# A decoder trunk on one core: the substitution of the delta rule's block inverses on the vector engine, and X without its mask

## The chip, the cores and the metric

The kernel runs on one core of one Trainium2 chip. The metric is the device time of one execution in microseconds; the runs of the kernel before are given by their median. The engines have short names throughout: PE is TensorE (PEld its weight loads), DVE is VectorE, ACT is ScalarE, POOL is GpSimd, SP is SyncE, whose queue issues the DMAs here.

## The reference

Two layers over 1024 tokens of 1024 features, all in float32. Layer 0 mixes tokens by a Conformer convolution (pointwise products with a gate, a causal depthwise convolution of width 31, a layer norm, a pointwise product), layer 1 by a gated DeltaNet with 8 heads of 128. After each mixer comes a squared-relu MLP with 4096 hidden features. Each part is preceded by an RMS norm, and one norm ends the whole. The change touches the delta rule of layer 1, which in the reference goes by chunks of 64 tokens:

```python
decay = jnp.exp(jnp.where(causal, g[..., :, None] - g[..., None, :], -jnp.inf))
k_beta = k * beta[..., None]
kk = jnp.einsum('bhnid,bhnjd->bhnij', k_beta, k) * decay
m = jnp.where(strict, kk, 0.0) + jnp.eye(CHUNK, dtype=jnp.float32)
rhs = jnp.concatenate([v * beta[..., None], k_beta * jnp.exp(g)[..., None]], axis=-1)
sol = lax.linalg.triangular_solve(m, rhs, left_side=True, lower=True, unit_diagonal=True)
```

`m` is 1 plus a strictly lower triangular matrix; the kernel forms its inverse instead of solving.

## The kernel before

The tokens go in two halves of 512. Activations lie with features on the partitions, 8 tiles of 128 x 512 to a half. A dense product (`product`, L164) takes 24 matmuls of 128 x 512: weights and activations are each the sum of two float32r parts, high and low, and three of the four combinations are added up (L178 to L180). Weights come from DRAM by SP (L130), ACT rounds the high part (L138, `wh`), and DVE subtracts to get the low one (L139, `wl`). This is done for every one of the 376 or so products, two ahead of their use.

The delta rule is work beside the products. It is written as generators that are advanced one step at every `tick()` inside and between the products: `gdn` runs `delta(hf, h0, yo)` for a pair of heads at a time, two streams of pairs, the second 40 steps behind the first, four pairs to a half. In the first half it goes beside the head projections (`gdn_in`) and the MLP of layer 0's second half, in the second half beside the projections and the MLP of layer 1's first half. The chunk here is 128 tokens, so a pair has 8 chunks (`NU`), each with a 128 x 128 matrix X.

What a pair does, in the names that the text uses:

- k and q are loaded (`ld`, DRAM tiles `sc` written by `gin`); sums of squares go to columns of `cl`.
- `e` is exp(-|difference of decay sums|) (L699 to L703, from `gr`, a load of the decay sums). POOL multiplies `e` by a strictly triangular mask into `el` (L706, `tril`) and by the other triangle in place (L708, `triu`).
- `X` is k times k, from PSUM, scaled and multiplied by `el` on DVE (L717). Its 32 x 32 diagonal blocks go to DRAM (`xd`, L722). `AT` (L731) is the same for q times k with `e`; POOL multiplies q by exp of the decays (L729, `qe`).
- The substitution: the 32 diagonal blocks of a pair are loaded with a block to a partition (`fx`, L742; `ft` begins as the identity, L743 and L744), and 31 steps on POOL turn `ft` into their inverses:

```python
for j in range(31):
    sh = [NU * 4, 31 - j, j + 1]
    nc.gpsimd.tensor_tensor(out=fm, in0=fx[:, j + 1:, j:j + 1].to_broadcast(sh),
                            in1=ft[:, j:j + 1, 0:j + 1].to_broadcast(sh), op=ALU.mult)
    nc.gpsimd.tensor_tensor(out=ft[:, j + 1:, 0:j + 1], in0=ft[:, j + 1:, 0:j + 1],
                            in1=fm, op=ALU.subtract)
```

- One pair is inverted at a time (the list `inverting`). `ft` goes to DRAM (`td`, L760) and comes back as `T` with rows on the partitions (L763). DVE transposes T's blocks (`ub`, L773) and copies them into `U` (L782, cleared before by POOL in L779). Matmuls y (L789, L798, L818, L825) make the rest of the 128 x 128 inverse from X, U and T, with copies of T by POOL (`t6s`, L811 to L813).
- The scan over the chunks (L832 on: `pk`, `R`, `py`, `ys`, `po`, `pS`, `st`) and the gated norm of the output, to DRAM (`yo`).

Every engine has one queue, and SP's queue issues all DMAs in order. The order in each queue isn't that of the source: a planner simulates a timeline of all engines from a cost for each instruction, with priorities by the order of the source (weights go 300 places earlier, `PRIO`), and writes the order down. On the chip each queue then keeps it, whatever the true durations are. Tiles come from pools with a fixed number of buffers; `g_tile` has 27.

Of the kernel before, what the change touches and what calls it, by code (L numbers as in the profile page):

```python
# [17 lines left out]
KC = D // P            # feature chunks  # L18
HT = S // 2            # tokens of a half
NCH = HT // P          # chunks of the delta rule in a half  # L20
H = 8                  # heads
NQ = 4                 # parts of the hidden layer
# [3 lines left out]
HG = 2                 # heads that go through the delta rule together  # L26
# how each tile of the depthwise convolution is done, by half (v: the vector engine, a: ScalarE
# and Pool, p: Pool, s: the vector engine but for the last SHARED taps), and how many taps go
# between two steps
# [3 lines left out]
INV = 5                # steps from the inverses to what uses them  # L33
IJ = 3                 # steps of the substitution traced at a time
LANE = 40              # steps by which the second stream of heads is behind
AHEAD = 2              # products whose weights are under way
PRIO = 300             # by how much weights go before what was traced earlier
HB = 10                # tiles in the pools
AB = 17
GB = 27  # L40
NB = 6                 # conv tiles of the second half before the first half's layer norm
# norms whose sum of squares goes to TensorE as two float32r parts
# [9 lines left out]
def _body(ctx, tc, a, out):  # L52
# [12 lines left out]
    def const(shape, name, val=None, dt=F32):  # L65
        t = cp.tile(shape, dt, tag=name, name=name)
        if val is not None:
# [10 lines left out]
    # [t, j] = 1 where t <= j, and its strict transpose  # L78
# [3 lines left out]
    tril = const([P, P], "tril")  # L82
    nc.gpsimd.affine_select(out=tril, in_=ones, pattern=[[-1, P]], compare_op=ALU.is_ge,
                            fill=0.0, base=-1, channel_multiplier=1)
# [13 lines left out]
    def split(dst, src):  # L98
        """src as the sum of two float32r parts"""
        nc.scalar.activation(out=dst[:, 0, :], in_=src, func=AF.Copy)  # L100
        nc.vector.tensor_tensor(out=dst[:, 1, :], in0=src, in1=dst[:, 0, :].bitcast(F32),  # L101
                                op=ALU.subtract)
# [7 lines left out]
    # weights that stay for a second pass over them  # L110
    keep = [f"m2_11_{NQ - 1}{o}" for o in range(KC)]

    def weights(src, name, n=KC * P):
        """weights as the sum of two float32r parts"""
        if n < KC * P:
            # few columns: both parts side by side
            raw = wp.tile([P, KC * P], F32, tag="raw", name=f"raw_{name}")
            nc.sync.dma_start(raw[:, :n], src)
            r3 = raw[:, :n].rearrange("p (k m) -> p k m", k=KC)
            both = wp.tile([P, KC * P], F32R, tag="wh", name=f"wh_{name}")  # L120
            b4 = both.rearrange("p (k i m) -> p k i m", k=KC, i=2)
            nc.scalar.activation(out=b4[:, :, 0], in_=r3, func=AF.Copy)
            nc.vector.tensor_tensor(out=b4[:, :, 1], in0=r3, in1=b4[:, :, 0].bitcast(F32),
                                    op=ALU.subtract)
            return both, None
        raw = wp.tile([P, KC * P], F32, tag="raw", name=f"raw_{name}")
        # the first ones in parts, so that the products start early
        n = KC * P // (2 if name in ("pa0_0", "pb0_0") else 1)
        for c in range(0, KC * P, n):
            nc.sync.dma_start(raw[:, c:c + n], src[:, c:c + n])  # L130
        kept = name in keep
        wh = wp.tile([P, KC * P], F32R, tag="kh" if kept else "wh", name=f"wh_{name}",
                     bufs=KC if kept else 2)
        wl = wp.tile([P, KC * P], F32R, tag="kl" if kept else "wl", name=f"wl_{name}",
                     bufs=KC if kept else 2)
        for c in range(0, KC * P, n):
            s = slice(c, c + n)
            nc.scalar.activation(out=wh[:, s], in_=raw[:, s], func=AF.Copy)  # L138
            nc.vector.tensor_tensor(out=wl[:, s], in0=raw[:, s], in1=wh[:, s].bitcast(F32),  # L139
                                    op=ALU.subtract)  # L140
        return wh, wl

    # work that goes on beside the products: it is traced in steps between them
# [41 lines left out]
    # the products in their order; weights are fetched and split one product ahead  # L185
# [38 lines left out]
    def add_stats(ps, x, first=True, last=True):  # L224
        """means over the features, with the tokens on the partitions, a chunk to a column"""
# [4 lines left out]
    def rstd_of_tokens(ps, name):  # L230
        """1 / sqrt(mean + eps) from such means, for all partitions with the tokens along them"""
# [26 lines left out]
    def norm(get, g, name, act, eng=nc.vector):  # L258
        """rms_norm of the half, split for the products, into act"""
# [13 lines left out]
    def norm_later(get, g, name, act):  # L273
        """rms_norm of the half but for 1 / rms, split into act; that factor is made meanwhile"""
# [88 lines left out]
    def own_taps(hf, ct):  # L363
        """how many taps of the tile are the vector engine's"""
        return {"v": CW, "s": CW - SHARED}.get(CONV[hf][ct][0], 0)
# [17 lines left out]
    def conv_pool(hf):  # L383
        """the taps that Pool adds up, by itself or from ScalarE's products"""
# [25 lines left out]
    def conv_vec(hf):  # L410
        """the vector engine's taps; the sum so far is in PSUM"""
# [27 lines left out]
    def layer_norm(hf, act):  # L439
# [8 lines left out]
        for k in range(KC):  # L448
            nc.vector.tensor_tensor(out=c[k], in0=c[k], in1=mu, op=ALU.subtract)
            sq = squares(c[k], f"ln{hf}{k}")  # L450
            # sums of two, or of all in the second half where TensorE has other work
# [57 lines left out]
    def mlp_out_last(l, hf, hid, q):  # L509
        """the end of the work: by quarters of the tokens, so that little is left after the last"""  # L510
# [38 lines left out]
    def ab(hf, act):  # L549
        """decays and betas of the half, tokens on partitions"""  # L550
        ps = dense(act, f"ab{hf}", 64)
        # rows 64.. have the share of the weights' low parts
# [15 lines left out]
        # what 1 + e rounded away  # L568
# [26 lines left out]
        # the sums of the decays with tokens along the row, for each head, in DRAM  # L595
# [8 lines left out]
    def gin(hf, act, h):  # L604
        """projections of a head, the short convolution, silu; to DRAM"""
# [38 lines left out]
    def delta(hf, h0, yo):  # L644
        """the delta rule for heads h0.. of the half; gated and normalised output into yo"""
# [44 lines left out]
        for i, h in enumerate(hh):  # L690
            # sums of the decays, the same on all partitions
# [12 lines left out]
            el = g_tile(f"el{nm}{h}")[:, :HT]  # L704
            el3 = el.rearrange("p (c d) -> p c d", c=NCH)
            nc.gpsimd.tensor_tensor(out=el3, in0=e3,  # L706
                                    in1=tril.unsqueeze(1).to_broadcast([P, NCH, P]), op=ALU.mult)
            nc.gpsimd.tensor_tensor(out=e3, in0=e3,  # L708
                                    in1=triu.unsqueeze(1).to_broadcast([P, NCH, P]), op=ALU.mult)
# [5 lines left out]
            X[h] = g_tile(f"X{nm}{h}")[:, :HT].rearrange("p (c d) -> p c d", c=NCH)  # L715
            for c in range(NCH):
                nc.vector.scalar_tensor_tensor(out=X[h][:, c, :], in0=g1[:, c, :],  # L717
                                               scalar=sk2[:, i, c:c + 1], in1=el3[:, c, :],
                                               op0=ALU.mult, op1=ALU.mult)
            for b in range(4):  # L720
# [18 lines left out]
        # inverses of the 32 x 32 diagonal blocks of 1 + X, a block to a partition  # L739
# [5 lines left out]
        for j in range(31):  # L745
# [3 lines left out]
            nc.gpsimd.tensor_tensor(out=fm, in0=fx[:, j + 1:, j:j + 1].to_broadcast(sh),  # L749
                                    in1=ft[:, j:j + 1, 0:j + 1].to_broadcast(sh), op=ALU.mult)  # L750
            nc.gpsimd.tensor_tensor(out=ft[:, j + 1:, 0:j + 1], in0=ft[:, j + 1:, 0:j + 1],  # L751
# [23 lines left out]
        # U is the transpose of the whole inverse: block by block  # L775
# [32 lines left out]
        # the inverse of the upper left quarter, not transposed  # L808
# [21 lines left out]
        # the scan  # L830
# [36 lines left out]
        # o is short of the factor rq / sqrt(dk); rec holds its square  # L867
# [42 lines left out]
    def final(hf, cols=slice(0, HT)):  # L910
# [18 lines left out]
        for k in range(KC):  # L929
            y = g_tile(f"fo{nm}{k}")[:, :n]  # L930
            if cols.start and k % 3 == 1:
                # the last ones are shared with Pool
# [21 lines left out]
    def gdn(hf, ready, yo, lane):  # L954
        """every other group of heads, once it has its inputs"""
# [87 lines left out]
def order(a):  # L1043
    """the products' names and weights, in their order"""
# [33 lines left out]
def arrange(i):  # L1078
    import numpy as np

    def cols(x):
        """[n * 128] -> [128, n]"""
        return np.asarray(x).reshape(-1, P).T
# [6 lines left out]
    def tiles(w):  # L1090
        """[K, N] -> [K / 1024 * N / 128, 128, 1024]: weights of 128 columns and 1024 rows"""
# [54 lines left out]
```

## Time and profile before

| | us |
|---|---|
| median of 3 runs | 2451.02 |
| lowest and highest run | 2450.73, 2455.44 |
| profiled execution, first to last instruction | 2454.3 |
| PE busy | 2333.6 |
| DVE busy | 1529.1 |
| ACT busy | 1082.7 |
| POOL busy | 973.5 |

The profile is of one execution, whose span is 3.3 us above the median of the runs. Lines named L are those of the kernel before. A row of a timeline gives the start, the duration, the engine, the line, the operation, what it writes and reads, and in brackets how long the engine was idle before it and what ended that.

### The profile page before, as it was taken

Reading aid. Unit: us, or ns where it says so; the run is one execution under the profiler, and the core shown is the slowest. Engines: PE = TensorE matmul, PEld = TensorE weight load, DVE = VectorE, ACT = ScalarE, POOL = GpSimd, SP = SyncE. Lnnn points to the kernel's source line nnn. Section 1 sums busy time; section 2 is a strip of 40 time slices with the busy share of each in tenths; the row PEclk is TensorE's granted clock in tenths of the full one; section 3 lists DMA queues with packets and bytes.
Section 4 is the critical chain, followed back from the end, with each engine's and each line's share of the span. In section 5 each row is a group of like instructions: output and inputs, shape, how many; then the busy total and the mean of one; then the engine's idle time right before and its main releaser. Section 6 shows DMA issues by size and latency. Waiting matters only on the chain. (4 is left out here: it accounts for less than half of the span.)

```text
span 2454.3 us, 30203 instructions
## 1 busy us (share of the span) xinstructions
PE 2333.6 (95%) x11412; PEld 1922.2 (78%) x11412; DVE 1529.1 (62%) x2166; ACT 1082.7 (44%) x1549; POOL 973.5 (40%) x945
## 2 busy tenths in 40 slices
PE   8798799999999989999999999899999999999998
PEld 6576677888778868888888888678888888788888
DVE  8998989645768765654435588656454346533334
ACT  6764442343536544443424365434334244432432
POOL 6898299999400557264300004571634000000000
PEclk9899899999999989999999999899999999999999
DMA  5222123333434533433325445334333243433332
GB/s 171 82 82 82 52 86 88 101 90 102 124 119 150 172 101 111 141 114 100 95 85 184 128 140 179 97 109 129 109 111 100 85 154 112 126 98 102 95 103 78
DMA packets 112962, 275.38 MB, mean 112 GB/s; under 512 B 28656, under 2 KB 30896, under 8 KB 112816
## 3 DMA queue, kind: packets, MB, share of 16 engines
q1 hardware_dynamic: 112816, 273.46, 36.6%
q8 instruction: 89, 1.46, 0.2%
q14 instruction: 57, 0.47, 0.1%
HBM read 241.92 MB, written 31.49 MB: 111 GB/s over the span
## 5 line engine op out<-in xcount | busy, mean ns | idle before, releaser
L138 ACT ACTIVATE wh_m<-raw_m 128x1024 fp32r<-128x1024 f32 x256 | 271.0, 1060 | 752.5 <-PE ps_m L179 698.0
L139 DVE TENSOR_TENSOR wl_m<-raw_m,wh_m 128x1024 fp32r<-128x1024 f32 x256 | 327.6, 1281 | 246.8 <-ACT wh_m L138 245.8
L180 PE MATMUL ps_m<-hid,wl_m 128*128 128x512 f32 (+1 forms) x1088 | 411.9, 380 | 6.8 <-DVE wl_m L139 6.8
L178 PE MATMUL ps_m<-hid,wh_m 128*128 128x512 f32 (+1 forms) x1088 | 413.5, 381 | 2.5 <-DVE xo L530 1.0
L179 PE MATMUL ps_m<-hid,wh_m 128*128 128x512 f32 (+1 forms) x1088 | 411.3, 379 | 0.0
L402 POOL TENSOR_TENSOR cp<-cp,cv 128x512 f32<-128x512 f32 x202 | 314.9, 1570 | 16.5 <-ACT cv L400 10.4
L180 PEld LDWEIGHTS ps_m<-hid,wl_m 128*128 128x128 f32 x1088 | 205.3, 189 | 47.2 <-DVE wl_m L139 10.5
L178 PEld LDWEIGHTS ps_m<-hid,wh_m 128*128 128x128 f32 x1088 | 205.3, 189 | 40.7 <-ACT wh_m L138 3.2
L179 PEld LDWEIGHTS ps_m<-hid,wh_m 128*128 128x128 f32 x1088 | 205.2, 189 | 37.0 <-issue 0.2
L935 POOL TENSOR_TENSOR fof<-fof,rstd_f 128x256 f32<-128x256 f32 x3 | 2.6, 890 | 567.8 <-DVE rstd_f L928 567.8
L729 POOL TENSOR_TENSOR ld<-qe,ld 128x512 f32<-128x512 f32 x16 | 21.7, 1356 | 482.3 <-ACT qe L696 254.2
L180 PE MATMUL ps_m<-xn_a,wl_m 128*128 128x512 f32 x512 | 202.9, 397 | 8.5 <-DVE wl_m L139 8.5
L180 PE MATMUL ps_m<-xn_b,wl_m 128*128 128x512 f32 x512 | 200.9, 393 | 5.9 <-DVE wl_m L139 5.9
L178 PE MATMUL ps_m<-xn_a,wh_m 128*128 128x512 f32 x512 | 201.9, 394 | 1.2 <-ACT wh_m L138 1.2
L178 PE MATMUL ps_m<-xn_b,wh_m 128*128 128x512 f32 x512 | 201.7, 394 | 1.0 <-ACT wh_m L138 1.0
L179 PE MATMUL ps_m<-xn_a,wh_m 128*128 128x512 f32 x512 | 201.3, 393 | 0.0
L179 PE MATMUL ps_m<-xn_b,wh_m 128*128 128x512 f32 x512 | 200.7, 392 | 0.0
L427 DVE SCALAR_TENSOR_TENSOR ca<-u,vec,ca 128x512 f32<-128x512 f32 x268 | 188.3, 745 | 0.5
L749 POOL TENSOR_TENSOR fm<-fx,ft 32x31 f32<-32x31 f32 (+15 forms) x248 | 163.6, 660 | 59.5 <-DMA fx<-xd 40.7
L751 POOL TENSOR_TENSOR ft<-ft,fm 32x31 f32<-32x31 f32 (+15 forms) x248 | 169.5, 683 | 19.4
L397 POOL TENSOR_SCALAR cv<-u,vec 128x512 f32<-128x512 f32 x90 | 174.2, 1943 | 0.0
L101 DVE TENSOR_TENSOR hid<-mt,hid 128x512 fp32r<-128x512 f32 x128 | 95.7, 748 | 48.4 <-ACT hid L100 48.2
(348 smaller groups left out, 4851.7 us busy)
## 6 DMA issues: line engine op xcount, KB each, us to landing
raw_m<-w SPq DMA_DIRECT2D x256, 512.0 KB, 3.6
raw_in<-w_in SPq DMA_DIRECT2D x64, 512.0 KB, 3.6
sc<-iy SPq DMA_DIRECT2D x64, 256.0 KB, 2.2
ld<-sc SPq DMA_DIRECT2D x64, 256.0 KB, 4.1
raw_p<-w_pw SPq DMA_DIRECT2D x16, 512.0 KB, 3.6
raw_go<-w_out SPq DMA_DIRECT2D x16, 512.0 KB, 3.6
raw_pa<-w_pw SPq DMA_DIRECT2D x15, 512.0 KB, 3.6
raw_pb<-w_pw SPq DMA_DIRECT2D x15, 512.0 KB, 3.6
```

What stands on the lines that cost most here:

```text
L101: nc.vector.tensor_tensor(out=dst[:, 1, :], in0=src, in1=dst[:, 0, :].bitcast(F32), op=ALU.subtract)
L138: nc.scalar.activation(out=wh[:, s], in_=raw[:, s], func=AF.Copy)
L139: nc.vector.tensor_tensor(out=wl[:, s], in0=raw[:, s], in1=wh[:, s].bitcast(F32), op=ALU.subtract)
L178: nc.tensor.matmul(o, wh[:, s], hi, start=(k == 0), stop=False)
L179: nc.tensor.matmul(o, wh[:, s], lo, start=False, stop=False)
L180: nc.tensor.matmul(o, wl[:, s], hi, start=False, stop=last)
L397: nc.gpsimd.tensor_scalar(out=t, in0=u[:, j:j + HT], scalar1=tap(ct, j), scalar2=None, op0=ALU.mult)
L402: nc.gpsimd.tensor_tensor(out=c, in0=c, in1=t, op=ALU.add)
L427: nc.vector.scalar_tensor_tensor(out=c if j == CW - 1 else acc, in0=u[:, j:j + HT], scalar=tap(ct, j), in1=acc, op0=ALU.mult, op1=ALU.add)
L729: nc.gpsimd.tensor_tensor(out=qT[h], in0=qe, in1=qT[h], op=ALU.mult)
L749: nc.gpsimd.tensor_tensor(out=fm, in0=fx[:, j + 1:, j:j + 1].to_broadcast(sh), in1=ft[:, j:j + 1, 0:j + 1].to_broadcast(sh), op=ALU.mult)
L751: nc.gpsimd.tensor_tensor(out=ft[:, j + 1:, 0:j + 1], in0=ft[:, j + 1:, 0:j + 1], in1=fm, op=ALU.subtract)
```

## The change

The two instructions of each substitution step are given to DVE. The mask `tril` and the tile `el` go: X is formed with `e` itself, and the multiplication by `triu`, which is done in place, comes after X in the source. Comments and docstrings go too.

```diff
-    tril = const([P, P], "tril")
-    nc.gpsimd.affine_select(out=tril, in_=ones, pattern=[[-1, P]], compare_op=ALU.is_ge,
-                            fill=0.0, base=-1, channel_multiplier=1)
...
             nc.scalar.activation(out=e, in_=e, func=AF.Exp, scale=-1.0)
-            el = g_tile(f"el{nm}{h}")[:, :HT]
-            el3 = el.rearrange("p (c d) -> p c d", c=NCH)
-            nc.gpsimd.tensor_tensor(out=el3, in0=e3,
-                                    in1=tril.unsqueeze(1).to_broadcast([P, NCH, P]), op=ALU.mult)
-            nc.gpsimd.tensor_tensor(out=e3, in0=e3,
-                                    in1=triu.unsqueeze(1).to_broadcast([P, NCH, P]), op=ALU.mult)
             yield
...
             for c in range(NCH):
                 nc.vector.scalar_tensor_tensor(out=X[h][:, c, :], in0=g1[:, c, :],
-                                               scalar=sk2[:, i, c:c + 1], in1=el3[:, c, :],
+                                               scalar=sk2[:, i, c:c + 1], in1=e3[:, c, :],
                                                op0=ALU.mult, op1=ALU.mult)
+            nc.gpsimd.tensor_tensor(out=e3, in0=e3,
+                                    in1=triu.unsqueeze(1).to_broadcast([P, NCH, P]), op=ALU.mult)
...
-            nc.gpsimd.tensor_tensor(out=fm, in0=fx[:, j + 1:, j:j + 1].to_broadcast(sh),
+            nc.vector.tensor_tensor(out=fm, in0=fx[:, j + 1:, j:j + 1].to_broadcast(sh),
                                     in1=ft[:, j:j + 1, 0:j + 1].to_broadcast(sh), op=ALU.mult)
-            nc.gpsimd.tensor_tensor(out=ft[:, j + 1:, 0:j + 1], in0=ft[:, j + 1:, 0:j + 1],
+            nc.vector.tensor_tensor(out=ft[:, j + 1:, 0:j + 1], in0=ft[:, j + 1:, 0:j + 1],
                                     in1=fm, op=ALU.subtract)
```

## Rows read from the trace of the kernel before

**Rows 1.** The page's first part: busy time, share of the span and number of instructions of each engine.

```profile
PE 2333.6 (95%) x11412; PEld 1922.2 (78%) x11412; DVE 1529.1 (62%) x2166; ACT 1082.7 (44%) x1549; POOL 973.5 (40%) x945
```

**Rows 2.** Waits of PE from 780 to 1250 us, longest first: who waited for whom, us in total, times, longest.

```profile
PE y L789 <- DVE U L782: 11.3, 1, 11.3
PE ps_m L180 <- DVE wl_m L139: 5.9, 3, 2.7
```

**Rows 3.** The same from 1530 to 1970 us.

```profile
PE y L789 <- DVE U L782: 10.6, 1, 10.6
PE ps_m L180 <- DVE wl_m L139: 8.3, 2, 5.7
PE py L849 <- DVE R L844: 2.0, 1, 2.0
```

**Rows 4.** Timeline of POOL from 832 to 890 us: the first substitution's first and last instruction (62 in all) and what follows.

```profile
832.74 0.25 POOL L749 TENSOR_TENSOR fm<-fx,ft 32x31 f32<-32x31 f32 x1 [9.04 <-DMA fx<-xd]
...
883.15 0.24 POOL L751 TENSOR_TENSOR ft<-ft,fm 32x31 f32<-32x31 f32 x1
...
886.38 1.25 POOL L706 TENSOR_TENSOR el<-e,tril 128x512 f32<-128x512 f32 x1
```

**Rows 5.** Timeline of DVE from 872 to 893 us.

```profile
887.67 1.12 DVE L717 SCALAR_TENSOR_TENSOR X<-g,cl,el 128x128 f32<-128x128 f32 x4 [11.07 <-POOL el L706]
888.98 0.45 DVE L773 STREAM_TRANSPOSE ub<-T 128x256 f32<-128x256 f32 x1 [0.18 <-DMA T<-td]
```

**Rows 6.** Stretches behind three pauses of PE, from its first matmul to the one at which the clock is back: length, busy time of PE, PEld, DVE, ACT and POOL, granted clock as a share of 2.4 GHz, DMA share, GB/s.

```profile
891.20:897.10 5.90, 5.68 (x45) 4.84 (x46) 4.19 (x12) 1.34 (x3) 1.28 (x1) 0.50 0.63 198
1568.80:1576.20 7.40, 7.15 (x49) 6.03 (x50) 5.56 (x12) 1.34 (x3) 1.28 (x1) 0.50 0.62 184
1657.10:1661.70 4.60, 4.58 (x13) 3.81 (x14) 3.12 (x5) 2.02 (x4) 0.00 (x0) 0.50 0.61 189
```

**Rows 7.** Timeline of POOL from 1602 to 1653 us: the second substitution of the second half.

```profile
1602.83 0.24 POOL L749 TENSOR_TENSOR fm<-fx,ft 32x31 f32<-32x31 f32 x1 [4.99 <-DMA fx<-xd]
...
1608.54 1.36 POOL L749 TENSOR_TENSOR fm<-fx,ft 32x156 f32<-32x156 f32 x1
1609.98 0.56 POOL L751 TENSOR_TENSOR ft<-ft,fm 32x156 f32<-32x156 f32 x1
...
1649.52 0.24 POOL L751 TENSOR_TENSOR ft<-ft,fm 32x31 f32<-32x31 f32 x1
```

**Rows 8.** Timeline of DVE from 1594 to 1658 us, beside the same substitution.

```profile
1595.23 1.13 DVE L717 SCALAR_TENSOR_TENSOR X<-g,cl,el 128x128 f32<-128x128 f32 x4 [1.53 <-PE g L714]
...
1608.32 1.23 DVE L139 TENSOR_TENSOR wl_in<-raw_in,wh_in 128x1024 fp32r<-128x1024 f32 x1
...
1655.52 0.45 DVE L773 STREAM_TRANSPOSE ub<-T 128x256 f32<-128x256 f32 x1 [12.07 <-DMA T<-td]
1655.88 1.18 DVE L139 TENSOR_TENSOR wl_m<-raw_m,wh_m 128x1024 fp32r<-128x1024 f32 x1
```

**Rows 9.** Waits of SP's queue over the whole span.

```profile
SPq L760 <- POOL ft L751: 95.1, 8, 15.6
```

**Rows 10.** The page's groups of instructions: line, engine, operation, what it writes and reads, shapes, count, then busy us and mean ns of one, then idle time before them.

```profile
L427 DVE SCALAR_TENSOR_TENSOR ca<-u,vec,ca 128x512 f32<-128x512 f32 x268 | 188.3, 745 | 0.5
L749 POOL TENSOR_TENSOR fm<-fx,ft 32x31 f32<-32x31 f32 (+15 forms) x248 | 163.6, 660 | 59.5 <-DMA fx<-xd 40.7
L751 POOL TENSOR_TENSOR ft<-ft,fm 32x31 f32<-32x31 f32 (+15 forms) x248 | 169.5, 683 | 19.4
```

**Rows 11.** Groups of DVE's instructions by shape from 1965 to 2320 us, where POOL does nothing.

```profile
L139 DVE TENSOR_TENSOR wl_m<-raw_m,wh_m 128x1024 fp32r<-128x1024 f32 x56 | 68.6, 1226 | 86.3 <-ACT wh_m L138 86.3
L101 DVE TENSOR_TENSOR hid<-mt,hid 128x512 fp32r<-128x512 f32 x31 | 21.4, 691 | 15.7 <-ACT hid L100 15.7
```

**Rows 12.** Timeline of DVE from 982 to 984 us: two small instructions of a chain, the second reading what the first wrote.

```profile
982.88 0.20 DVE L876 RECIPROCAL cl<-cl 128x8 f32<-128x8 f32 x1
983.11 0.17 DVE L877 TENSOR_TENSOR cl<-cl 128x8 f32<-128x8 f32 x1
```

**Rows 13.** Groups of DVE's instructions by shape from 832 to 884 us, beside the first substitution.

```profile
L626 DVE SCALAR_TENSOR_TENSOR iy<-ir,vec,iy 128x512 f32<-128x512 f32 x18 | 16.0, 891 | 0.3
L139 DVE TENSOR_TENSOR wl_in<-raw_in,wh_in 128x1024 fp32r<-128x1024 f32 x7 | 10.0, 1430 | 7.2 <-ACT wh_in L138 7.2
```

**Rows 14.** A stretch of the convolution and two of the first half's projections, columns as in rows 6.

```profile
61.00:122.00 61.00, 45.03 (x159) 34.49 (x160) 60.75 (x68) 43.41 (x66) 54.69 (x36) 0.86 0.26 82
736.00:797.00 61.00, 61.00 (x283) 50.32 (x282) 53.81 (x92) 39.71 (x59) 0.00 (x0) 1.00 0.48 149
797.00:921.00 124.00, 111.44 (x598) 91.76 (x597) 91.70 (x165) 64.65 (x87) 65.65 (x81) 0.94 0.45 136
```

**Rows 15.** Waits of DVE from 780 to 1250 us.

```profile
DVE ub L773 <- DMA T<-td: 28.9, 4, 10.6
DVE AT L731 <- PE g L728: 5.7, 4, 2.1
DVE ld L886 <- DMA ld<-sc: 2.8, 2, 1.4
```

**Rows 16.** POOL's other instructions in the delta rule, by line: shortest, median and longest in ns, first and last start, shapes.

```profile
L706 POOL TENSOR_TENSOR el<-e,tril x16: 1252/1301/2066, 808.1 to 1805.6; 128x512 f32<-128x512 f32 x16
L812 POOL COPY t6s<-T x8: 386/388/390, 888.6 to 1874.9; 32x256 f32<-32x256 f32 x8
```

## The prediction

> **What bounds the kernel now.** I read the page's engine table first: PE is busy 2333.6 of 2454.3 us, DVE 1529.1, POOL 973.5 [rows 1]. The matmuls are not touched, so all that the change can give or take is PE's idle time and its time at a low clock. Next comes where PE waits in the two stretches in which the delta rule runs beside the products (780 to 1250 us and 1530 to 1970 us). One cause stands above the rest: the matmul y of L789, which needs U, waited 11.3 us in the first half and 10.6 us in the second; then come waits for split weights, 5.9 us in three and 8.3 us in two, and 2.0 us for R [rows 2, 3]. That is 38.1 us; everything else there is under a microsecond.
>
> Why is U late? The timeline of the first of the eight substitutions tells it. POOL begins at 832.74 and ends at 883.39 us, 50.7 us for 62 instructions, and only then can its queue go on to the next pair's el, at 886.38 [rows 4]. DVE stands 11.07 us until 887.67, because its next instruction, X, needs that el; ub, from which U is copied, stands behind X in DVE's queue [rows 5]. PE has y at the head of its own queue, long before U is there. Three queues with a written order stand still, because one engine was slower than the order assumed. The clock pays too: granted 0.50 (1.2 GHz) for 5.9 and 7.4 us behind the two pauses, and for 4.6 us behind a third [rows 6].
>
> The other six substitutions do the same on a smaller scale. In the second half's second case the last ft ends at 1649.76 [rows 7]; ub comes at 1655.52, after a DVE pause of 12.07 us, and the split of the next weights right behind it [rows 8]. That is PE's wait of 5.7 us [rows 3]. SP's queue suffers as well: its store td waited 95.1 us for POOL's ft in the eight cases [rows 9], with loads of weights behind it.
>
> **The change, part by part.** Moved are 8 x 62 = 496 tensor_tensor instructions on 32 partitions. On POOL they are 163.6 + 169.5 = 333.1 us, 660 and 683 ns each [rows 10]. Their sizes are (31-j)(j+1) elements, 31 to 256, mean 176. None stands on DVE, so I interpolate between DVE's tensor_tensor of 512 elements, 691 ns, and one of 8, 170 ns [rows 11, 12]: 1.03 ns per element, and 170 + 168 x 1.03 = 343 ns for 176. Each needs the one before it. In a chain of dependent small ones on DVE the starts are 0.23 us apart where the first lasts 0.20 [rows 12], so 0.03 us goes between: 0.373 x 62 = 23.1 us for a substitution. The ends: at the price of the 8 elements, 0.20 x 62 = 12.4 us; stretched like L626 beside POOL (891 ns against 745) [rows 10, 13], 27.7. All are well under POOL's 50.7 and 46.9 us [rows 4, 7], even with other DVE work in the gaps. DVE's total grows by 8 x 23.1 = 185 us to some 1710.
>
> Some of that comes back. While POOL ran the first substitution, 18 of L626 took 891 ns and 7 splits 1430 [rows 13], against 745 for the same shape at L427 [rows 10] and 1226 for the split where POOL was quiet [rows 11]: 18 x 0.146 + 7 x 0.204 = 4.1 us. POOL was held up too: the fm that met the split at 1608.32 took 1.36 us, the ft of the same size behind it 0.56 [rows 8, 7].
>
> Can DVE hold the rest? The projection stage is the tight one. At 736 to 797 us DVE is busy 53.81 of 61 us, 88%, and PE has no idle time; from 797 to 921 it is busy 91.7 of 124 us [rows 14]. With 23.1 more and 4 less that is 110.8, 89%; but if PE's pause goes, the stage is some 14 us shorter, and DVE is full. What PE needs of DVE are only the splits, 1.2 us per product; the short convolution's taps can wait until the stage is over, where DVE has room. That is the cover; without it all of those 14 us are given back in each half, 28. I take 4 us in all, nearer to nothing because of the stretch at 88%.
>
> New waits: the first fm waits in DVE's queue for the load fx, with weight splits queued behind. The nearest row is DVE's wait for another load, ld: at most 1.4 us [rows 15]. So 0 to 8 x 1.4 = 11 us of pauses; DVE's 28.9 us of pauses before ub [rows 15] became 5.9 us at PE [rows 2]. I take 3 us, a little over that ratio. ub still follows ft by the store td and the load T, 5.8 us from 1649.76 to 1655.52; the pause before it shrinks to what the order misjudges.
>
> The mask: 16 multiplications into el of 1.3 us leave POOL's queue [rows 16], 21 us. X no longer waits for them, but its long waits were POOL's queue and are counted above. The one by triu now stands behind X, since it writes e in place: POOL's queue waits for DVE there, with qe's product, the memsets of U and the copies of t6s behind it. AT waits 1.3 us after X for triu, where it had to wait for its matmul anyway, 5.7 us in four [rows 15], 1.4 each; nothing either way, and at worst 16 x 1.3 = 21 us of DVE pauses, 4 us at PE by the ratio above, if that cover fails. What X now holds on and above the diagonal is read by nobody: the substitution reads rows below, and U is zero where the matmuls would meet the rest. One constant less at the start: nothing.
>
> The sum, against the profiled execution: the long waits, 11.3 + 10.6 = 21.9. The slow clock behind them costs half of 5.9 + 7.4 us [rows 6], 6.6. The small waits are 5.9 + 8.3 + 2.0 = 16.2, with half of 4.6 us at the slow clock behind the longest: 18.5. Of these I take half, 9.3, since the path through td and T stays. Against it 4 and 3. 21.9 + 6.6 + 9.3 - 7 = 30.8: 2454.3 becomes 2423.5. The median of the runs is 2451.0, 3.3 below that span, so I forecast 2420. A change of less than 0.2%, 5 us, can't be told from none here.
>
> Ends of this case: all of the 18.5 back at no cost is 47.0, 2404; and 2399 with some relief of DVE beside. With both costs at their ends (11 and 28) the first rivals begin.
>
> A rule of the Trainium skill would take more. Rows first: a POOL instruction that met a DVE split lasted as long as the split [rows 7, 8]. "SBUF — State Buffer", section "SBUF: two separate sides", says that a VectorE instruction with two SBUF inputs and a GpSimd one that reads SBUF lock the shared ports in turn, the later one blocked for the other's whole length. By it the moved instructions would stand behind POOL's remaining triu, qe and t6s work, an estimate of 6.0 us per pair (two of each at 1.3, 1.3 and 0.39 us [rows 16], triu and qe being of el's shape); at the 5.9 in 28.9 above, 48 us would cost PE 10, and the sum would be 2430, within the likeliest case. No run shows it yet for these instructions.
>
> **Rivals.**
> *Waits in DVE's queue take the place of POOL's (0.15).* If the order has the first fm as though fx came at once, DVE stands 6.5 us per pair, from X's end at 1596.36 to POOL's start at 1602.83 [rows 8, 7]. Such a pause costs PE between 1.3 (by 5.9 in 28.9) and 3 us (by 5.7 for 12.07); at 2 that is 16. The small waits stay as well: 21.9 + 6.6 - 16 = 12, so 2439; 2433 to 2445. For it: ub's waits are of this kind [rows 15]. Against it: those for ld are short.
>
> *DVE becomes the bound, and the kernel slower (0.13).* In the convolution's stretch at 61 to 122 us, DVE is full and PE busy only 45.03 of 61 us [rows 14]. If splits come behind the chain in the projection stages, PE waits for DVE as it does there. It decides from 47 us on: of the 185 us moved, if over a quarter reaches PE, the whole gain is spent. A third is 62: 2451 + 15 = 2466. For it: DVE comes out full there by my own sum. Against it: the stretch at 88%.
>
> *No change (0.07).* The order is written anew as a whole, and y stands as early before a U that is late again, now by DVE; 2446 to 2456.
>
> **How the numbers follow.** The likeliest case, 2404 to 2433, has 0.65. With the first rival, faster has 0.80; within 0.2%, 0.07; slower, 0.13. The range for 8 in 10 goes from the likeliest case's lower end with relief to the end of the first rival: 2399 to 2445.
>
> **What would show it.** The 62 instructions of a pair should stand on DVE at about 0.34 us each and be done in 23 to 35 us; POOL should be busy about 973 - 333 - 21 = 619 us and DVE 1680 to 1714; PE's waits for U should be under 3 us; td's wait for ft on SP far under 95 us; the clock 1.00 from 797 to 921 us, where it was 0.94 [rows 14]. The prediction is wrong if PE's waits for splits in the delta stretches pass the 14 us of now, if DVE pauses over 3 us before a first fm, or if the time before 780 us, where nothing of the moved work lies, changes by more than 5 us.

## The result, and the profile after

| | before | after |
|---|---|---|
| median of the runs, us | 2453.23 (4 runs) | 2428.43 (4 runs) |
| lowest and highest | 2450.73, 2457.30 | 2427.12, 2430.01 |
| profiled execution, first to last instruction | 2454.3 | 2428.0 |

The kernel became faster: the ratio is 0.990, with a 95% interval of 0.9886 to 0.9914. That is 24.8 us, where 31 were forecast (2420; the range was 2399 to 2445). The size is near; the reason given for the larger part of it is not what the trace shows.

The page's first line, to be held against [rows 1]:

```profile
PE 2325.6 (96%) x11412; PEld 1917.6 (79%) x11412; DVE 1647.8 (68%) x2662; ACT 1088.2 (45%) x1551; POOL 617.2 (25%) x432
```

Waits of PE from 780 to 1250 us, and below them those from 1530 to 1970 us [rows 2, 3]; line numbers are now six lower in this part:

```profile
PE y L783 <- DVE U L776: 7.5, 1, 7.5
PE tkv L656 <- DMA ld<-sc: 2.3, 1, 2.3
PE y L819 <- DVE y3s L815: 0.9, 1, 0.9
...
PE y L783 <- DVE U L776: 6.1, 1, 6.1
PE ps_m L177 <- DVE wl_m L136: 0.8, 1, 0.8
PE py L843 <- DVE R L838: 0.2, 1, 0.2
```

The waits for split weights are all but gone (14.2 us before, 0.8 now); `tkv` (the transpose of v, behind a load) and `y3s` (DVE's copy between two of the y) wait a little more than before. The two long waits for U, which were to vanish, only shrank, from 11.3 to 7.5 and from 10.6 to 6.1 us. They stand at the first pair of each half, as before.

The timeline of DVE at that first pair: the first and last instructions of the substitution (62 in all), one between, and what follows. Below it POOL's instruction at 880 us and PE's y:

```profile
833.26 0.20 DVE L743 TENSOR_TENSOR fm<-fx,ft 32x31 f32<-32x31 f32 x1 [3.56 <-DMA fx<-xd]
...
880.58 1.45 DVE L743 TENSOR_TENSOR fm<-fx,ft 32x192 f32<-32x192 f32 x1
882.06 0.35 DVE L745 TENSOR_TENSOR ft<-ft,fm 32x192 f32<-32x192 f32 x1
...
888.40 0.17 DVE L745 TENSOR_TENSOR ft<-ft,fm 32x31 f32<-32x31 f32 x1
890.58 1.22 DVE L136 TENSOR_TENSOR wl_in<-raw_in,wh_in 128x1024 fp32r<-128x1024 f32 x1 [2.01 <-ACT wh_in L135]
896.04 0.45 DVE L767 STREAM_TRANSPOSE ub<-T 128x256 f32<-128x256 f32 x1 [4.24 <-DMA T<-td]
...
880.15 1.68 POOL L712 TENSOR_TENSOR e<-e,triu 128x512 f32<-128x512 f32 x1 [6.22 <-ACT wh_in L135]
...
897.18 0.28 PE L783 MATMUL y<-U,X 64*32 64x32 f32 x2 [7.50 <-DVE U L776]
```

The substitution takes 55.3 us here, 833.26 to 888.57; POOL took 50.7 [rows 4]. y itself runs at 897.18; before, PE came back from its pause at 891.20 [rows 6]. So U lets y run 6 us *later* than before, and PE waits 3.8 us less, since PE itself comes to y 9.8 us later. Most of that is y's place in PE's queue: 139.3 products (of 24 matmuls) come before it, 138.0 before the change; in the second half 243.7 against 242.3. At some 5.4 us for a product that is 7 us of matmuls moved ahead of y. The costs by which the order was written are not known here; that it comes close to DVE's time and was short of POOL's is an inference, which e2, e4, e5 and e13 below test.

Why the chain is so long there, the windows tell (columns as in rows 6): the first pair's substitution, and the stretch of [rows 14] once more. The second fence has a later pair's first and last instruction.

```profile
833.00:889.00 56.00, 56.00 (x261) 46.33 (x260) 53.08 (x128) 26.46 (x34) 2.67 (x3) 1.00 0.50 161
...
797.00:921.00 124.00, 113.22 (x620) 93.81 (x619) 101.71 (x226) 67.52 (x89) 14.69 (x15) 0.97 0.45 142
```

```profile
1121.03 0.19 DVE L743 TENSOR_TENSOR fm<-fx,ft 32x31 f32<-32x31 f32 x1 [0.71 <-DMA fx<-xd]
...
1155.91 0.18 DVE L745 TENSOR_TENSOR ft<-ft,fm 32x31 f32<-32x31 f32 x1
```

DVE is busy 53.08 of 56 us at the first pair, so that the 62 instructions stand in gaps of the short convolution and the splits. The first pair of the second half needs 53.8 us. The other six pairs need 35 to 47 us (35.1 here), where POOL needed 43 to 48, and PE waits for U at none of them.

The moved instructions and the short convolution's taps, as groups (columns as in rows 10), then two of DVE's waits from 780 to 1250 us [rows 15] and SP's wait with the store td over the whole span [rows 9]:

```profile
L623 DVE SCALAR_TENSOR_TENSOR iy<-ir,vec,iy 128x512 f32<-128x512 f32 x144 | 109.8, 768 | 0.8
L743 DVE TENSOR_TENSOR fm<-fx,ft 32x31 f32<-32x31 f32 (+15 forms) x248 | 83.5, 337 | 20.4 <-DMA fx<-xd 15.2
L745 DVE TENSOR_TENSOR ft<-ft,fm 32x31 f32<-32x31 f32 (+15 forms) x248 | 81.3, 328 | 5.1
...
DVE ub L767 <- DMA T<-td: 11.3, 4, 4.2
DVE fm L743 <- DMA fx<-xd: 7.6, 4, 3.6
...
SPq L754 <- DVE ft L745: 15.8, 6, 3.8
```

The price of one instruction was well forecast (343 ns; 337 and 328). SP's wait fell from 95.1 to 15.8 us, DVE's before ub from 28.9 to 11.3.

By stages (the first from the first matmul of its half's decay product to the first of its output product, the second from the first matmul of its decay product to the last of its output product): the first half's stage went from 633.1 to 623.1 us, the second's from 650.6 to 632.2; all ahead of the first changed by +1.2 us, what lies between by nothing, and the end by +0.9. Within the two stages PE's idle time fell by 22.5 us, and the time lost to the slower clock (busy time multiplied by the missing share of the clock) by 5.2.

### The profile page after: what moved, and what is told of

It reads as the page before. It is cut to its first block, busy times and chain, and to the rows that moved or that the text cites. A ratio compares the mean times of both kernels' runs of the same rounds, so it can differ in the third digit from the quotient of the medians.

```text
span 2428.0 us, 30172 instructions
## 1 busy us (share of the span) xinstructions
PE 2325.6 (96%) x11412; PEld 1917.6 (79%) x11412; DVE 1647.8 (68%) x2662; ACT 1088.2 (45%) x1551; POOL 617.2 (25%) x432
## 5 line engine op out<-in xcount | busy, mean ns | idle before, releaser
L399 POOL TENSOR_TENSOR cp<-cp,cv 128x512 f32<-128x512 f32 x202 | 310.8, 1550 | 17.7 <-ACT cv L397 11.7
L315 DVE TENSOR_TENSOR hn<-hn,ps_m 128x512 f32<-128x512 f32 x56 | 38.4, 686 | 110.8 <-PE ps_m L177 110.6
L175 PEld LDWEIGHTS ps_m<-xn_b,wh_m 128*128 128x128 f32 x512 | 96.2, 188 | 21.8 <-ACT wh_m L135 1.8
```

What stands on the lines that cost most here:

```text
L175: nc.tensor.matmul(o, wh[:, s], hi, start=(k == 0), stop=False)
L315: nc.vector.tensor_tensor(out=hs[hf][o], in0=hs[hf][o], in1=ps, op=ALU.add)
L399: nc.gpsimd.tensor_tensor(out=c, in0=c, in1=t, op=ALU.add)
```

## The experiments

All are compared with the kernel before, which stood at 2452.8 to 2453.3 us beside them. The stages are those just named, from the profiled execution.

| kernel | median us | ratio, 95% interval | first stage | second stage |
|---|---|---|---|---|
| before | 2453.2 | 1 | 633.1 | 650.6 |
| after | 2428.4 | 0.990 [0.9886, 0.9914] | 623.1 | 632.2 |
| e1_move_only | 2437.7 | 0.9932 [0.9917, 0.9946] | 624.3 | 637.4 |
| e2_mask_only | 2465.7 | 1.0044 [1.0029, 1.0060] | 642.9 | 646.5 |
| e4_before_inv9 | 2471.3 | 1.0069 [1.0052, 1.0085] | 643.2 | 654.0 |
| e3_after_inv9 | 2423.2 | 0.9872 [0.9858, 0.9887] | 619.3 | 630.0 |
| e7_inv9_ft2 | 2422.5 | 0.9876 [0.9861, 0.9890] | 619.1 | 628.9 |
| e8_const_kept | 2428.4 | 0.9898 [0.9883, 0.9913] | 624.0 | 632.1 |
| e5_fm_twice | 2448.1 | 0.9982 [0.9973, 0.9991] | 631.4 | 643.8 |
| e6_first_pool | 2448.4 | 0.9980 [0.9971, 0.9989] | 634.0 | 639.9 |
| e12b_tap_act5 | 2425.9 | 0.9886 [0.9869, 0.9902] | 620.5 | 632.4 |
| e12_tap_act | 2421.7 | 0.9873 [0.9858, 0.9887] | 616.7 | 629.3 |
| e13_pool_beside | 2504.3 | 1.0213 [1.0198, 1.0229] | 661.7 | 671.4 |
| e11_pool_busy | 2722.6 | 1.1098 [1.1077, 1.1119] | 622.0 | 632.6 |

### The two halves of the change, each alone

e1_move_only is the kernel before with the two instructions of the substitution on DVE; `el` and `tril` stay on POOL.

```diff
-            nc.gpsimd.tensor_tensor(out=fm, ...
+            nc.vector.tensor_tensor(out=fm, ...
-            nc.gpsimd.tensor_tensor(out=ft[:, j + 1:, 0:j + 1], ...
+            nc.vector.tensor_tensor(out=ft[:, j + 1:, 0:j + 1], ...
```

> The substitution on DVE, the mask of X kept (el and tril stay on POOL). If the gain comes from the move, this has nearly all of it: 2425 to 2434 us, PE's two long waits for U 5 to 9 us each, the waits for weights in the delta stretches gone. If a good part comes from the mask (X no longer behind POOL's el), it loses that part: 2436 to 2445 us, and DVE waits for el by more than 10 us in all.

e2_mask_only is the changed kernel with these two back on POOL.

> The mask dropped, the substitution still on POOL. If the gain comes from the move alone: 2446 to 2458 us, long waits for U of 11 us and more in both halves (y of the first pair stands here after 137.5 products, 0.5 earlier than before), small waits of 10 us and more kept. If DVE's stand before X was itself a cause: 2436 to 2444 us, since X no longer waits for el.

The move alone brings 15 us. Its time is that of the second expectation, though DVE waits only 5.9 us for el. Dropping the mask alone costs 13, slower than either expectation, and with the move done it brings 9 more: it is not the nothing that the sum had for it, and its sign depends on the move. (The profiled executions show 6.3 of the 13: that of e2 is the fastest of its runs, that of the kernel before one of the slower.) What the mask alone does stands in PE's waits from 780 to 1250 us, then in the queues of SP (DMA issues) and DVE and ACT:

```profile
PE ps_in L175 <- ACT wh_in L135: 10.5, 1, 10.5
...
862.36 0.33 SPq L127 DMA_DIRECT2D raw_in<-w_in  x1
880.52 0.34 SPq L754 DMA_DIRECT2D td<-ft  x1
880.91 0.41 SPq L690 DMA_DIRECT2D gr<-gcd  x1
...
884.39 0.69 DVE L696 TENSOR_TENSOR e<-gr,cols 128x512 f32<-128x512 f32 x1 [12.56 <-DMA gr<-gcd]
...
884.43 1.28 ACT L693 ACT_TABLE_LOAD   x1 [14.40 <-DMA gr<-gcd]
```

No wait for U is left at y, yet PE stands as long: X no longer stops for POOL, so SP's queue reaches td first and stops there for POOL's last ft, 880.26 + 0.24; the next pair's load gr is right behind td, ACT and DVE stand for gr, and the split of the weights behind them. POOL's substitution is as late as ever (653 and 677 ns an instruction); the pause has only gone to another queue. Why the whole is slower than before, and not the same, these lines don't tell.

e4_before_inv9 asks the same in another way: the kernel before, but what uses the inverses is traced nine steps after them.

```diff
-INV = 5
+INV = 9
```

> The kernel before (substitution on POOL, mask kept) with 9 steps in place of 5. The order has y of the first pair after 139.8 products, not 138.0, 10 us later. If the gain of the change in the first pairs was y's place alone and not DVE's speed, the long waits fall to 1 to 3 us here too and the time to 2430 to 2438 us, with the small waits of 10 to 16 us kept. If DVE's speed is needed, the long waits stay at 7 us or more: 2444 us or more.

PE's waits from 780 to 1250 us, and one of DVE's from 860 to 915 us:

```profile
PE ps_m L180 <- DVE wl_m L139: 10.8, 3, 4.7
PE ps_in L180 <- DVE wl_in L139: 9.6, 1, 9.6
PE y L789 <- DVE U L782: 2.6, 4, 0.9
...
DVE X L717 <- POOL el L706: 12.3, 1, 12.3
```

y's wait is gone here too, and the kernel is 18 us slower: the next pair's el still stands behind the substitution in POOL's queue, X waits 12.3 us for it, and a split of weights behind X. Here, placing the use later doesn't cure a producer that comes late: the pause moves.

e8_const_kept is the changed kernel with the unused constant `tril` back, to see how much a small edit moves the written order.

> The changed kernel with the constant tril still made at the start by POOL, used by nobody. It tells how far the time moves when the order is written anew around something that costs nothing: within 2 us of the changed kernel (2426 to 2431 us) if the 9 us between it and the kernel with only the substitution moved are the mask's own; 4 us or more if a part of those 9 us is order.

It is the changed kernel to 0.01 us in the median, so an edit outside the delta rule doesn't move the time. How far an order moves that loses 16 instructions of the rule itself, it can't tell. Of the 10.0 us between the spans of e1 and the changed kernel the stages account for 6.4 (in the second the waits for U are 9.0 us in four against 6.1 in one); 3.6 lie ahead of and behind the stages, where the kernels are alike; the stretch ahead alone varies from 723.7 to 726.7 us among the runs of this kind here. Through what the mask brings the 6.4 is not shown beyond these waits.

### What is left at the first pair

e3_after_inv9 is the changed kernel with `INV = 9`; e7_inv9_ft2 gives `ft` a second buffer besides.

> The changed kernel with 9 steps in place of 5 between an inverse and its use. The order then has y of the first pair after 141.3 products, not 139.3, 11 us later. If the two waits of 7.5 and 6.1 us that the changed kernel has left are a matter of y's place in the order, they go, and half the slow clock with them: 2408 to 2416 us. If they come from DVE being full in the projections, so that U is always late by what PE gains, 4 us or more of each stays: 2422 to 2430 us.

```diff
-INV = 5
+INV = 9
-        ft = wp.tile([NU * 4, 32, 32], F32, tag="ft", name=f"ft{nm}", bufs=1)
+        ft = wp.tile([NU * 4, 32, 32], F32, tag="ft", name=f"ft{nm}", bufs=2)
```

> The changed kernel with 9 steps from the inverse to its use (as in the run that gave 2423.2 us) and two buffers for ft, so that the next pair's substitution need not wait for POOL's clearing of ft behind the store of the last one (DVE stood 4.4 us for that). If that stand makes U late, PE's two waits of 5.3 and 3.9 us for U shrink by 2 us or more each: 2416 to 2421 us. If it is the loads fx and T alone: 2421 to 2425 us.

With the substitution on DVE the same edit that cost 18 us now brings 5; y's waits are 5.3 and 3.9 us, not nothing. In e3 a first fm waited 4.4 us for POOL to clear `ft`. The second buffer doesn't change the time, so that wait isn't what holds it. The first pair's substitution in e3, first and last instruction:

```profile
832.86 0.20 DVE L743 TENSOR_TENSOR fm<-fx,ft 32x31 f32<-32x31 f32 x1 [3.25 <-DMA fx<-xd]
...
899.67 0.18 DVE L745 TENSOR_TENSOR ft<-ft,fm 32x31 f32<-32x31 f32 x1
```

It takes 67.0 us, 11.7 more than in the changed kernel: y stands two products later (some 11 us), and the new order filled that time with other work between the links. The chain is longer and the wait shorter, so the chain's length by itself is not what PE pays; PE pays for what U is late against y's place.

e5_fm_twice does the multiplication of every step twice, unused work of 82 us on DVE.

```diff
+            nc.vector.tensor_tensor(out=fm, in0=fx[:, j + 1:, j:j + 1].to_broadcast(sh),
+                                    in1=ft[:, j:j + 1, 0:j + 1].to_broadcast(sh), op=ALU.mult)
```

> The changed kernel with each multiplication of the substitution done twice on DVE: 248 more instructions of about 0.35 us, 87 us in all, which the order takes into account (y of the later pairs stands 2.4 to 4.9 products later, y of the first pairs at the same place). If the gain is that the order fits the true durations on DVE, most of it stays: 2430 to 2440 us, PE's waits grow only at the two first pairs, whose y can't move, from 7 to 10 to 16 us. If the gain is that DVE ends the substitution sooner, it is lost with the longer chain: 2445 us or more, and waits of PE for weights in the delta stretches come back to 10 us and more.

PE's waits from 780 to 1250 and from 1530 to 1970 us, and the first pair's first and last instruction:

```profile
PE y L785 <- DVE U L778: 18.3, 1, 18.3
...
PE y L785 <- DVE U L778: 18.2, 1, 18.2
...
834.18 0.20 DVE L743 TENSOR_TENSOR fm<-fx,ft 32x31 f32<-32x31 f32 x1 [3.28 <-DMA fx<-xd]
...
901.89 0.18 DVE L747 TENSOR_TENSOR ft<-ft,fm 32x31 f32<-32x31 f32 x1
```

A pair gets 10.3 us more of DVE's work. At the first pairs, where y stays at its place, that comes out in full: the substitution grows from 55.3 to 67.9 us and the waits from 7.5 and 6.1 to 18.3 and 18.2. At the other six pairs the order puts y later, and no wait for U arises: 62 us of added work cost PE nothing there. The time is that of the second expectation, but the waits for weights, its other sign, stay at 0.4 us. Work on DVE that the order reckons with is paid only where the use can't move, at the first pair of each half.

e6_first_pool then gives just these first pairs back to POOL, so that DVE has room.

```diff
+        eng = nc.gpsimd if h0 == 0 else nc.vector
...
-            nc.vector.tensor_tensor(out=fm, ...
+            eng.tensor_tensor(out=fm, ...
-            nc.vector.tensor_tensor(out=ft[:, j + 1:, 0:j + 1], ...
+            eng.tensor_tensor(out=ft[:, j + 1:, 0:j + 1], ...
```

> The changed kernel with the first pair of each half substituted on POOL again, the other six on DVE. It parts the gain: if the six later pairs make most of it, the time is 2434 to 2442 us, with pauses of PE of 10 us and more at each first pair (for U, or for whatever then stands behind POOL) and none at the others. If DVE's being full at the first pairs costs more than POOL's lateness there, it is faster than the changed kernel: 2418 to 2426 us.

PE's waits from 780 to 1250 and from 1530 to 1970 us:

```profile
PE ps_in L175 <- ACT wh_in L135: 10.8, 1, 10.8
...
PE ps_in L175 <- ACT wh_in L135: 10.6, 1, 10.6
```

It misses what was expected, on the slow side: 20 us slower than the changed kernel. The pauses of e2 are back, and POOL needs 701 and 725 ns for an instruction. From e2 to e6 the six later pairs bring 17 us, from e6 to the changed kernel the two first ones 20. Even with DVE full and the chain longer, the first pairs are better on DVE, as long as the mask is dropped.

e12b_tap_act5 takes work from DVE instead: the first tap of the short convolution goes to ACT. e12_tap_act has this and `INV = 9`.

```diff
-                nc.vector.tensor_scalar(out=y, in0=r[:, 0:HT], scalar1=w(0), scalar2=None, op0=ALU.mult)
+                nc.scalar.activation(out=y, in_=r[:, 0:HT], func=AF.Copy, scale=w(0))
```

> The changed kernel with the first tap of the short convolution (0.47 us on DVE, three in four projections) on ACT instead, and nothing else changed: y of the first pairs stands at the same place, after 139.3 and 243.7 products. If PE's waits for U are left over because DVE is full in the projections, they shrink from 7.5 and 6.1 us to 2 to 4 us, as some 4 to 5 us of DVE's work go from beside each first pair: 2416 to 2424 us. If it is the loads fx and T alone, they stay: 2426 to 2431 us.

> The same with 9 steps from the inverse to its use. If both causes (y's place and DVE's load) add up, the waits for U go to 0 to 2 us: 2410 to 2419 us. If they are one and the same, no better than either alone: 2419 to 2424 us.

PE's waits in e12b, in the same two windows:

```profile
PE y L782 <- DVE U L775: 2.8, 1, 2.8
PE y L818 <- DVE y3s L814: 2.3, 1, 2.3
...
PE y L782 <- DVE U L775: 4.2, 1, 4.2
PE y L818 <- DVE y3s L814: 2.0, 1, 2.0
```

The waits for U shrink, as a full DVE asks for, but waits for y3s come up, and only 2.5 us of time are won, within the intervals. With both edits no wait for U above 0.2 us is left in the first half, 0.4 in the second, and the kernel stands at 2421.7 us: the best of all here with e7 and e3, which it doesn't beat beyond its interval, 7 us under the changed kernel and 32 under the one before. The waits went as if y's place and DVE's load added up, the time as if they were one: with e3's 9.2 us of waits for U gone, PE's idle time in the two stages fell by only 4 us, since smaller waits took their place.

### Does POOL stretch DVE?

e13_pool_beside adds two POOL multiplications to each step of the changed kernel, which read what DVE's instruction wrote and whose result is not used.

```diff
+            for i in range(2):
+                no = wp.tile([NU * 4, 256], F32, tag="no", name=f"no{nm}{j}{i}", bufs=2)
+                no = no[:, :sh[1] * sh[2]].rearrange("p (i j) -> p i j", j=j + 1)
+                nc.gpsimd.tensor_tensor(out=no, in0=fm, in1=fx[:, j + 1:, 0:j + 1], op=ALU.mult)
```

> The changed kernel, and two POOL multiplications behind each step of the substitution, of fm and fx into a scratch tile that nobody reads (fm has 8 buffers for it): POOL works beside DVE's substitution as it did before the change. The order of PE's matmuls around y is that of the changed kernel. If the engines stretch each other, which the order doesn't know, the mean of DVE's two instructions goes from 333 ns to over 400, PE's waits for U grow to 10 us and more and the time to 2440 us or more. If DVE isn't stretched by POOL: 2426 to 2432 us.

DVE's groups from 780 to 1970 us, and its timeline beside POOL's at the first pair:

```profile
L745 DVE TENSOR_TENSOR ft<-ft,fm 32x31 f32<-32x31 f32 (+15 forms) x248 | 134.6, 543 | 5.1
L743 DVE TENSOR_TENSOR fm<-fx,ft 32x31 f32<-32x31 f32 (+15 forms) x248 | 123.9, 500 | 31.2 <-DMA fx<-xd 15.8 <-DVE ft L745 0.5
...
854.68 0.39 DVE L745 TENSOR_TENSOR ft<-ft,fm 32x240 f32<-32x240 f32 x1
855.00 0.66 DVE L615 COPY tails<-ir 128x3 f32<-128x3 f32 x1
...
857.48 0.88 DVE L745 TENSOR_TENSOR ft<-ft,fm 32x247 f32<-32x247 f32 x1
...
853.76 2.53 POOL L750 TENSOR_TENSOR no<-fm,fx 32x240 f32<-32x240 f32 x2 [0.41 <-DVE fm L743]
857.03 2.52 POOL L750 TENSOR_TENSOR no<-fm,fx 32x247 f32<-32x247 f32 x2 [0.75 <-DVE fm L743]
```

The same DVE instructions take 500 and 543 ns where they took 337 and 328. POOL is at work beside both of the ft shown: the one that takes 0.39 us begins as a split of weights ends (853.54 to 854.75), beside which a POOL instruction had been stretched to 1.88 us; the one that takes 0.88 begins inside a running POOL instruction. So not every meeting costs DVE time.

Taken over the 496, the time above the shortest of each shape is 95 us, and nearly all of it, 94.7 us, lies on the 451 that began while a POOL instruction was running; 119 of these lost less than 0.06 us each. PE waits again for U (10.0 and 9.6 us) and for splits (17 us at `wl_in` and `wl_m` in the first half's stretch), and the kernel is 2.1% slower than before.

The same count in the kernel before: of the 83 us that POOL's 496 instructions took above their shortest, 80.0 lie on the 205 that began while a DVE instruction was running, 2.0 on the 233 beside which DVE did nothing. The stretch goes both ways, and it is dear on the side that bounds.

e11_pool_busy was the first try at this, with POOL's dummies reading a constant.

```diff
+                nc.gpsimd.tensor_tensor(out=no, in0=vec[:NU * 4, 0:256], in1=vec[:NU * 4, 128:384], op=ALU.mult)
```

> The changed kernel, and beside each step of the substitution two POOL multiplications of 32 x 256 elements from a constant into a scratch tile that nobody reads: as many instructions on POOL as before the change, with the order of PE's matmuls as in the changed kernel. If the two engines stretch each other (the cause of POOL's being late before), DVE's substitution and splits now take longer than the order has them, and PE's pauses come back: 2440 us or more, the mean of L743 and L745 over 400 ns. If what counted was only that POOL's queue was blocked for the next pair, the time goes up by POOL's queue too, but DVE's durations stay at 330 ns. If neither counts, 2426 to 2432 us.

It failed as an experiment on the substitution: the dummies had nothing to wait for, so the order put all 496 ahead of the delta rule, a stretch that grew by 295 us. One of DVE's subtractions and POOL's last instruction beside it:

```profile
274.84 24.35 DVE L136 TENSOR_TENSOR wl_pb<-raw_pb,wh_pb 128x1024 fp32r<-128x1024 f32 x1 [8.79 <-ACT wh_pb L135]
...
297.39 0.71 POOL L749 TENSOR_TENSOR no<-vec 32x256 f32<-32x256 f32 x1
```

It stood for 24.35 us, while POOL went through 24 instructions without a gap, and ended 1.1 us after the last of them; the shortest of its shape takes 1.21. The 17 for `wl_pb` took 3456 ns in the mean, 1548 in the kernel before, and this one makes most of the difference. The delta rule's stages stayed as in the changed kernel, so it says nothing on them.

## Why the prediction was right, and where its steps were not

**The bound and the cause: right.** PE's idle time and slow clock are 27.7 of the 28.4 us that the two stages gave back (2.1 were lost outside them), and the origin is POOL's lateness. If every one of the 496 instructions of the kernel before had taken the shortest duration that its shape shows, a pair would have needed 31.2 us of POOL and not 41.6; at the first pair of each half the difference is 14.7 and 13.6 us, beside pauses of 11.3 and 10.6. On DVE the same count gives 19.7 against 20.6. That the order reckoned with some such undisturbed pace is an inference. e2 and e4 show that the pause is POOL's and not y's: without the wait at y it stands in SP's queue behind td (e2), or in DVE's before X (e4).

**"The long waits, 11.3 + 10.6 = 21.9", all back: mis-sized.** They gave 8.3. The step that failed is the length of a substitution, "23 to 35 us": it was taken at DVE's bare pace, while at the first pairs DVE is full, and it took 55.3. The text had seen "DVE is full" there, and put 4 us on it, since the taps could wait. They didn't: the instructions of the chain lie between taps. So U is no earlier in its stage than before, and the gain at y came with y's later place. The waits of the changed kernel are 7.5 and 6.1 us, where under 3 was forecast. Beside the first, DVE itself stood still for 3.56 us until fx came and for 4.24 until T came, 7.8 in all; but e12b has 6.7 us of such stands beside a wait of 2.8, so how the 7.5 part between the loads and DVE's load stays open.

**Half of the small waits: mis-sized the other way.** Of the 16.2 us, 15 are gone; 2.6 came with `tkv` and `y3s`. The later pairs have the room that the first lack. The long waits were 13.6 us too high in the sum, the small ones 7 too low, and the two costs took 7 off: that the sum of 30.8 us stands so near the 26.3 between the spans is in good part luck.

**The slow clock:** 5.2 us came back, where 6.6 and a part of the small waits' share were forecast. From 797 to 921 us the clock was 0.97 and not 1.00: it was 0.50 for 6.8 us from 895 us on, at the pause that remains.

**The mask "nothing either way": wrong.** It is +13 us alone and -9 with the move. The sum priced its instructions; in e2 what counts is which queue meets POOL's ft first, and the -9 is not fully explained.

**The busy times:** POOL's 617.2 us was forecast as 619. DVE's 1647.8 lies under 1680 to 1714. The durations of its other work fell by 31 us, near the 33 assumed (the taps from 833 to 768 ns); but neighbouring records overlap at their ends (an instruction that starts at 862.97 for 0.73 us is followed by one at 863.63), so 165 us of durations add less to the busy time.

**The rivals.** *Waits in DVE's queue* came in part: 15.2 us for fx in eight, longest 3.9, past the 3 us named as a sign against the forecast, while the time kept to it; the sign was set too tight. *DVE becomes the bound* is near the truth at two of the eight pairs; e5 prices more work there one for one, and at nothing where y can move. It never came near the 47 us from which it would decide. *No change:* y does stand before a U that is later than before, but y's place moved with it.

**The rule of the Trainium skill.** A DVE instruction was held by POOL's work: the fm at 880.58 took 1.45 us beside the `triu` product at 880.15, where the ft of the same size behind it takes 0.35. "SBUF — State Buffer" of the Trainium skill, section "SBUF: two separate sides", states this lock: the one that starts first keeps the shared ports for its whole length. The 80.0 of 83 us on POOL's side before and the 94.7 of 95 us on DVE's side in e13 agree with it, though not every meeting cost time. As a price for this change it was too high: over all eight pairs DVE's 496 instructions took 7.2 us more than at the shortest durations of their shapes, and 2.3 of these lie on the four that began beside a running POOL instruction; 48 would follow if every one of POOL's remaining instructions held them up.

## What to carry to other kernels

Where queues follow a written order, ask of an engine not only how long its instructions take, but by how much its result is later than the place of its use: that difference comes out as a pause at whichever queue meets the result first, and with POOL late, placing the use later only moved the pause (e4). A moved chain's length is its duration plus all that its new queue puts between its links; take it from the busy share of the very stretch (here 53 of 56 us), not from the instruction's price. A small edit to what waits for a late engine can have either sign, so price it with the other edit and without.

## What had not been expected of the hardware

POOL's instructions stretch even a DVE copy of 128x3 with a single input: 0.15 to 0.17 us in 23 of 24 cases of the changed kernel, 0.66 beside a running POOL instruction in e13. And a DVE instruction can be kept out by many of POOL's in a row: 24.35 us for a subtraction of at best 1.21, while POOL worked without a gap (e11).
